# RWKV and RG-LRU blocks of the first stage: the short block first instead of last, three parts that end with the thirds of the tokens, and each part's chained part finished within the part

## The chip, the cores and the metric

The kernel runs on one core of a Trainium2 chip. The metric is the time of one execution on the device in microseconds, the median over several runs. One execution was recorded by the hardware profiler; its trace gives a start and a duration for each instruction on the five engines: TensorE (PE; PEld are its weight loads), VectorE (DVE), ScalarE (ACT), GpSimd (POOL) and SyncE (SP, which here issues the DMAs).

## The reference

One layer over 2064 tokens (16 learned ones ahead of 2048), model width 1024, all in fp32:

```
p  = rms_norm(h, norm_mix_pre) @ w_in
oa = rg_lru_group(xa, ya, ...)              # width 256: conv of 4, two gates, a linear scan over tokens
ob = forgetting_attention_group(q, k, v, f) # 8 heads of 64, causal, with a decay per head
oc = rwkv7_group(pc, ...)                   # 4 heads of 64, state S (64 x 64) per head:
#   S = S * w_t - (S kk_t) (kk_t a_t)^T + v_t k_t^T ;  o_t = S r_t ;  then group norm, bonus, gate
h  = h + rms_norm(concat([oa, ob, oc]) @ w_out, norm_mix_post)
f  = causal_dwconv(rms_norm(h, norm_ffn_pre) @ ffn_up, ffn_conv)     # width 2 x 2816
h  = h + rms_norm((gelu(gate) * val) @ ffn_down, norm_ffn_post)
```

`oa` and `oc` are recurrences over the tokens; everything else is matrix work.

## The kernel before

**First stage.** The tokens are cut into three thirds, which end at tokens 784, 1552 and 2064, each of two blocks of columns (400 + 384, 384 + 384, 256 + 256). For each third the tokens are normalised and transposed (line 145 is the transpose on TensorE, line 132 the last step of the norm on VectorE), and then projected through `w_in` in units of 128 output columns. A projection unit is made of split products, three matmuls for each fp32 one (lines 177 to 179), into the PSUM tile `psp`; there are 1152 of them in each third by the program. Lines 296 and 297 are the forget gate's small projection (`psf`).

**Recurrences beside it.** RWKV runs in nine blocks, b0 to b8, of chunks of 64 tokens: `Rwkv.block(b)` is a generator, and a step of it is what lies between two `yield`s. Block b begins at token `start(b)`. b0 to b7 have four chunks and b8 has one. A block has two parts. The first goes up to `SOLVED`: the block's *front* (loads, line 1075 the decay's products, 1105 the keys' normalisation, 1126 the bonus), the *scores* of each chunk (1149, 1154, with the transposes of line 1185), and the *rounds* that solve 16 x 16 triangles, 15 on GpSimd (line 1204) and VectorE (1205) by turns. The second, called here the block's *ending* (e0 to e8), is the chained part: it reads the solved triangles back (1218), combines them in many 32 x 32 matmuls (1234), forms the chunks' products (1278 to 1322), carries the state from chunk to chunk (1330 on TensorE, 1334 on VectorE) into the outputs (1361, 1366), normalises them (1371 to 1398, with lines 1386 and 1390 on TensorE) and stores them (1400). PSUM tiles of the recurrences are `rps` and `eps`. Some tiles of the rounds exist once and are used again by the next block's front, so the matmul of line 1105 for block b+1 comes after the rounds of block b.

The function `recurrences` strings this together: for a third, two steps of gates, then for each of three blocks the part up to `SOLVED`, the *previous* block's ending (kept in `R.ending`), and the RG-LRU block of the same tokens (`lru_block`, lines 1474 to 1508, with matmuls 1481 and 1482). `Beside` advances it: from the fourteenth projection unit of each third it makes 1.25 steps for each block of columns of a unit, and what is left goes on in the next third. After the last third `beside.finish()` runs the rest and a loop runs the last ending.

**What comes next.** The recurrences' pools are closed and the attention starts (`Attn.run`). Its half 0 takes the first two blocks of 512 queries of all heads, its half 1 the others. Line 704 and 705 are scores (`sc`), 576 and 578 the products for the maxima (`mx`), 591 transposes, 727 the output (`po`), 783 and 784 the denominators. For half 1 a further key buffer (`k2`, a constant part filled by the casts of line 499 on VectorE, the keys loaded at lines 537 to 541) and small buffers (`mt`) lie in the memory that the recurrences' pools had. Then follow `w_out` and the feed-forward part.

**Order.** The program's text does not fix the order on an engine: a scheduler with a model of times reorders the instructions of the whole program within their dependences, and so score matmuls of the attention stand among the recurrences' last matmuls.

Of the kernel before, what the change touches and what calls it, by code (L numbers as in the profile page):

```python
# [21 lines left out]
META = 16  # L22
# [204 lines left out]


def w_in_step(core, pools, psum, weights, block, kind, c0, scr):

    nc = core.nc
# [217 lines left out]
class Attn:  # L449
# [54 lines left out]
    def next(self, s):  # L504
        self.turn[s] = (self.turn[s] + 1) % len(self.ring[s])
        return self.ring[s][self.turn[s]]
# [165 lines left out]
    def weights(self, h, b, keys, queries, fill):  # L672
# [19 lines left out]
        def group_scores(group):  # L692
# [23 lines left out]
            return out  # L716

        def group_values(group, ps_, start, end):

            if start:  # L720
# [194 lines left out]
CH = 64  # L915
# [87 lines left out]
class Rwkv:  # L1003
# [6 lines left out]
    @staticmethod  # L1010
    def start(b):

        return META - CH + 4 * CH * b

    def __init__(self, core, pool, dpool, psum, epsum, scr, k):
        self.core, self.pool, self.dpool, self.psum, self.epsum = core, pool, dpool, psum, epsum
# [28 lines left out]
            nc.vector.scalar_tensor_tensor(out, v(raw[:, p, :n]), k["mu"][:, cc], out, op0=ALU.mult, op1=ALU.add)  # L1045

    def block(self, b):
        nch = 4 if b < 8 else 1
        n = CH * nch
        m2 = 2 * nch  # L1050
        c0 = PAD + self.start(b)
        nc, k = self.nc, self.k
# [78 lines left out]
    def chunks(self, b, nch, sg, rav, bk, wc, bon):  # L1131
# [3 lines left out]
        nc, k, core = self.nc, self.k, self.core  # L1135
# [177 lines left out]


        st = k["st"]
        nc.vector.tensor_copy(st[:, 0], st[:, 4])
        gain = self.ps().rearrange("p (c a t) -> p c a t", a=2, t=64)
        for c in range(nch):
            for h in range(2):
# [793 lines left out]
def recurrences(core, R, lk, f_bias, scr, blocks, part):  # L2113


    for blk in blocks:
        gate_block(core, R, f_bias, scr, blk[2])
        yield
    for b in ((0, 1, 2), (3, 4, 5), (6, 7, 8))[part]:
        gen = R.block(b)  # L2120
        while next(gen) != R.SOLVED:
            yield
        yield from R.ending
        R.ending = gen
        yield from lru_block(core, R, scr, lk, b)


_INS = [
# [9 lines left out]
def hybrid_block_kernel(ctx: ExitStack, tc: tile.TileContext, args, out):  # L2138
    a = {s: v[0] if s != "meta_tokens" else v for s, v in args.items()}
    nc = tc.nc  # L2140
# [23 lines left out]
    with ExitStack() as p1:  # L2164
# [7 lines left out]
        with ExitStack() as p1a:  # L2172
# [6 lines left out]
            for part in range(3):  # L2179
# [10 lines left out]
                if part == 0:  # L2190
# [17 lines left out]
                    R = Rwkv(core, rp, dp, ps_rw, ps_ae, scr, rk)  # L2208
# [15 lines left out]
                if part < 2:  # L2224
                    following = w_in_norm(core, pools, ps_mm, x, meta, g_pre, part + 1)
        beside.finish()
        for _ in R.ending:
            pass
        rec.close()
        p2 = ExitStack()  # L2230
        ps_wo = [pool(p2, "ps_wo", 2, space=PSUM, **right)]
# [192 lines left out]
```

## Time and profile before

| | |
|---|---|
| median of 3 runs | 2971.63 us (2969.79 to 2985.59) |
| profiled execution | 2975.74 us, its span 2974.0 us |
| mean clock granted to TensorE | 0.979 of full speed |
| TensorE busy | 2852.4 us, 96% of the span |
| VectorE, ScalarE, GpSimd busy | 69%, 51%, 43% |
| first third's last projection matmul, next third's first | 284.9 us, 327.3 us |
| last projection matmul | 855.2 us |
| first matmul of the attention | 873.7 us |
| last matmul of the recurrences | 1091.9 us |
| first maxima of the attention's half 1 | 1104.0 us |

The times of the last four rows are starts, counted from the start of the span. A row of the trace names the engine, the line of the program and the operation, as out<-in with the tiles' names; fp32 matmuls leave two records each. In brackets stands how long the engine was idle before and what it waited for.

### The profile page before, as it was taken

To read this page: it belongs to the slowest core of one execution; us is meant where nothing else is said; L and a number is where in the kernel's file an instruction comes from. 1 tells how busy PE (TensorE), PEld (TensorE's weight loads), DVE (VectorE), ACT (ScalarE), POOL (GpSimd) and SP (SyncE) were. 2 spreads that over 40 slices of the span, in tenths; PEclk is the share of its full clock that TensorE was granted. 3 is DMA by queue.
4 is the path that set the end of the run, shared out by engine and by line. 5 is a ranking of instruction groups with operands and counts; after the bars stand their busy time and mean duration, and the time that the engine had idled before them with its cause. 6 is when DMAs were issued, how large, how long until landed. Compare 5 with 4: busy or idle time off the path is not lost.

```text
span 2974.0 us, 53306 instructions
## 1 busy us (share of the span) xinstructions
PE 2852.4 (96%) x18826; PEld 2444.3 (82%) x18826; DVE 2039.5 (69%) x3977; ACT 1503.8 (51%) x2937; POOL 1285.9 (43%) x1555
## 2 busy tenths in 40 slices
PE   6999999999988889999999999999999999999998
PEld 6998899888866555666568999999999999787887
DVE  5257754665677775566656998888778787646766
ACT  4246432554346655455644665666565665324333
POOL 1001121132114566667722667455655444646443
PEclk9999899999988999999999999999999999999999
DMA  6776479576653358445245665577777764436453
GB/s 216 237 231 220 144 250 320 182 245 218 217 125 81 88 116 229 106 98 136 64 130 189 203 193 175 165 230 211 208 211 219 218 198 138 150 114 221 146 173 121
DMA packets 470344, 530.52 MB, mean 178 GB/s; under 512 B 86862, under 2 KB 356888, under 8 KB 468524
## 3 DMA queue, kind: packets, MB, share of 16 engines
q1 hardware_dynamic: 469308, 526.18, 58.8%
q8 instruction: 148, 2.42, 0.3%
q14 instruction: 120, 0.98, 0.1%
q0 software_dynamic: 768, 0.93, 0.1%
HBM read 368.07 MB, written 158.90 MB: 177 GB/s over the span
## 4 chain that ended last, share of the span: by engine, by line
PE 75%; DVE 8%; DMA 7%; ACT 4%; issue 2%; POOL 2%; SPq 1%; DVEq 0%; POOLq 0%; ACTq 0%
PE psu L177 9%; PE psu L178 9%; PE psu L179 9%; PE psp L179 4%; PE psp L178 4%; PE psp L177 4%; PE psd L177 4%; PE psd L178 4%; PE psd L179 4%; PE po L727 4%; PE pswo L177 2%; PE pswo L178 2%; PE pswo L179 2%; PE sc L704 2%; PE mx L576 2%
## 5 line engine op out<-in xcount | busy, mean ns | idle before, releaser
L178 PE MATMUL psu<-xo,uw 128*128 128x344 f32 x1848 | 591.5, 320 | 0.0
L177 PE MATMUL psu<-xo,uw 128*128 128x344 f32 x1848 | 586.2, 322 | 2.4 <-DVE vb L1889 1.9
L179 PE MATMUL psu<-xo,uw 128*128 128x344 f32 x1848 | 582.0, 320 | 0.3 <-DVE uw L1698 0.3
L177 PE MATMUL psp<-xh,wh 128*128 128x384 f32 (+2 forms) x1152 | 378.7, 329 | 1.4 <-DMA wh<-scr_wk 1.0
L179 PE MATMUL psp<-xh,wl 128*128 128x384 f32 (+2 forms) x1152 | 376.8, 328 | 0.6 <-DMA wl<-scr_wk 0.6
L178 PE MATMUL psp<-xl,wh 128*128 128x384 f32 (+2 forms) x1152 | 375.3, 326 | 0.0
L1698 DVE TENSOR_TENSOR uw<-uq,uw 128x512 fp32r<-128x512 f32 x341 | 320.2, 944 | 59.1 <-ACT uw L1697 55.9
L177 PEld LDWEIGHTS psu<-xo,uw 128*128 128x128 f32 x1848 | 345.9, 188 | 4.2 <-DVE vb L1889 3.0
L178 PEld LDWEIGHTS psu<-xo,uw 128*128 128x128 f32 x1848 | 347.2, 188 | 0.0
L179 PEld LDWEIGHTS psu<-xo,uw 128*128 128x128 f32 x1848 | 345.7, 188 | 1.1 <-DVE uw L1698 1.1
L1697 ACT ACTIVATE uw<-uq 128x512 fp32r<-128x512 f32 x462 | 288.1, 627 | 94.8 <-PE psu L179 44.9
L709 ACT ACTIVATE p<-sc,bias 128x512 f32<-128x512 f32 (+4 forms) x352 | 197.5, 589 | 172.1 <-PE sc L705 142.1
L581 DVE TENSOR_REDUCE mc<-mx 128x1 f32<-128x512 f32 (+6 forms) x352 | 190.7, 567 | 116.7 <-PE mx L576 77.5
L1837 DVE SCALAR_TENSOR_TENSOR uy<-psu,ffn_cols,uy 128x342 f32<-128x342 f32 (+1 forms) x390 | 220.9, 568 | 60.3 <-ACT uy L1835 58.6
L1845 POOL TENSOR_TENSOR uy<-uy,uy 128x342 f32<-128x342 f32 (+1 forms) x132 | 145.1, 1099 | 232.5 <-DVE uy L1837 61.0
L1698 POOL TENSOR_TENSOR uw<-uq,uw 128x512 fp32r<-128x512 f32 x121 | 183.1, 1513 | 133.3 <-ACT uw L1697 111.9
L179 PEld LDWEIGHTS psp<-xh,wl 128*128 128x128 f32 x1152 | 218.6, 190 | 8.9 <-issue 6.2
L177 PEld LDWEIGHTS psp<-xh,wh 128*128 128x128 f32 x1152 | 218.4, 190 | 8.4 <-issue 4.4
L178 PEld LDWEIGHTS psp<-xl,wh 128*128 128x128 f32 x1152 | 218.3, 189 | 7.2 <-issue 5.7
L748 POOL TENSOR_TENSOR acc<-acc,p 128x512 f32<-128x512 f32 (+3 forms) x186 | 198.8, 1071 | 46.8 <-ACT p L709 21.3
L1698 DVE TENSOR_TENSOR fo<-u,fo 128x896 fp32r<-128x896 f32 x88 | 101.6, 1154 | 130.9 <-ACT fo L1697 130.3
L1697 ACT ACTIVATE fo<-u 128x896 fp32r<-128x896 f32 x88 | 81.3, 923 | 207.1 <-PE psd L179 116.0
(490 smaller groups left out, 6339.4 us busy)
## 6 DMA issues: line engine op xcount, KB each, us to landing
uq<-scr_us SPq DMA_DIRECT2D x220, 256.0 KB
uq<-in_ffn_up_dram SPq DMA_DIRECT2D x209, 256.0 KB
wl<-scr_wk SPq DMA_DIRECT2D x48, 512.0 KB
wh<-scr_wk SPq DMA_DIRECT2D x48, 512.0 KB
u<-scr_ff SPq DMA_DIRECT2D x88, 256.0 KB
scr_ff<-uy SPq DMA_DIRECT2D x110, 171.0 KB
raw<-in_w_in_dram SPq DMA_DIRECT2D x24, 512.0 KB
scr_wk<-wh SPq DMA_DIRECT2D x24, 512.0 KB
```

What stands on the lines that cost most here:

```text
L177: nc.tensor.matmul(out, ah, bh, start=first, stop=False, skip_group_check=more)
L178: nc.tensor.matmul(out, ah, bl, start=False, stop=False, skip_group_check=more)
L179: nc.tensor.matmul(out, al, bh, start=False, stop=last, skip_group_check=more)
L576: nc.tensor.matmul(ps[:rows, : e - a], q3[:, qo : qo + rows], k2[:, a:e], start=True, stop=not last)
L581: self.reduced = nc.vector.tensor_reduce(mc[:rows, i, ci : ci + 1], ps[:rows, : e - a], axis=AX.X, op=ALU.max)
L709: last = nc.scalar.activation(p[:rows, :w], ps[:rows, :w], AF.Exp, bias=bias[:rows, j : j + 1])
L727: mm = nc.tensor.matmul(po[at : at + 64, c0:n], v1[:rows, j], p[:rows, : n - c0], start=start and i < 2, stop=end and i + 2 >= len(group), ...
L748: eng.tensor_tensor(a, ps_[0][0][:rows, c0:n] if start and i == 1 else a, p[:rows, : n - c0], op=ALU.add)
L1697: core.nc.scalar.activation(hi, src, AF.Copy)
L1698: (eng or core.nc.vector).tensor_tensor(lo, src, hi, op=ALU.subtract)
L1837: core.conved = stt(y[:, :n], src[:, i : n + i], cw[:, 44 * i + cc : 44 * i + cc + 1], y[:, :n], op0=ALU.mult, op1=ALU.add)
L1845: core.pooled = nc.gpsimd.tensor_tensor(v[:, :n], g[:, :n], v[:, :n], op=ALU.mult)
```

## The change

The short block of one chunk becomes b0 instead of b8. Blocks 1 to 8 have four chunks each and begin at tokens 16, 272, ... 1808, so that b3 ends at token 784, b6 at 1552 and b8 at 2064, where the thirds end. The state is copied on from column 1 after the short block. The three parts of `recurrences` have four, three and two blocks instead of three each, and each part ends with the ending of its last block; before, that ending was left for the next part, or for the loop behind the last one, which goes. In steps the parts have 74, 56 and 38 instead of 46, 56 and 56 with 10 behind them.

```diff
@@ -1010,7 +1010,7 @@
     @staticmethod
     def start(b):
 
-        return META - CH + 4 * CH * b
+        return META + 4 * CH * (b - 1) if b else META - CH
 
     def __init__(self, core, pool, dpool, psum, epsum, scr, k):
         self.core, self.pool, self.dpool, self.psum, self.epsum = core, pool, dpool, psum, epsum
@@ -1045,7 +1045,7 @@
             nc.vector.scalar_tensor_tensor(out, v(raw[:, p, :n]), k["mu"][:, cc], out, op0=ALU.mult, op1=ALU.add)
 
     def block(self, b):
-        nch = 4 if b < 8 else 1
+        nch = 4 if b else 1
         n = CH * nch
         m2 = 2 * nch
         c0 = PAD + self.start(b)
@@ -1313,7 +1313,7 @@
 
 
         st = k["st"]
-        nc.vector.tensor_copy(st[:, 0], st[:, 4])
+        nc.vector.tensor_copy(st[:, 0], st[:, 1 if b == 1 else 4])
         gain = self.ps().rearrange("p (c a t) -> p c a t", a=2, t=64)
         for c in range(nch):
             for h in range(2):
@@ -2116,13 +2116,15 @@
     for blk in blocks:
         gate_block(core, R, f_bias, scr, blk[2])
         yield
-    for b in ((0, 1, 2), (3, 4, 5), (6, 7, 8))[part]:
+    for b in ((0, 1, 2, 3), (4, 5, 6), (7, 8))[part]:
         gen = R.block(b)
         while next(gen) != R.SOLVED:
             yield
         yield from R.ending
         R.ending = gen
         yield from lru_block(core, R, scr, lk, b)
+    yield from R.ending
+    R.ending = ()
 
 
 _INS = [
@@ -2224,8 +2226,6 @@
                 if part < 2:
                     following = w_in_norm(core, pools, ps_mm, x, meta, g_pre, part + 1)
         beside.finish()
-        for _ in R.ending:
-            pass
         rec.close()
         p2 = ExitStack()
         ps_wo = [pool(p2, "ps_wo", 2, space=PSUM, **right)]
```

The change moves instructions at three places that matter for what follows. In the rows, `<-` stands between what is written and what is read, and xN counts matmuls in a row.

On TensorE between the first third's projection and the second's, before, in the middle of that place: `rps` rows of line 1234 and on are e0, with four chunks, `eps` rows of line 1075 are the front of b2, `pst` rows the transposes of the next tokens.

```order
L1234 MATMUL rps_2389<-rwxu_2339,rwsc_1646 32x32 x32
L1234 MATMUL rps_2465<-rwxu_2339 32x32 x16
L1234 MATMUL rps_2484<-rwxu_2339 32x32 x32
L1234 MATMUL rps_2558<-rwxu_2339,rwsc_1646 32x32 x16
L1075 MATMUL eps_3380<-rwwa_3361,wa_up 128x256 x2
L1234 MATMUL rps_2623<-rwxf_2387,rwxu_2339 32x32 x16
L1278 MATMUL rps_2642<-rww_202_1647,rwsc_1646 64x64 x16
L1075 MATMUL eps_3386<-rwwa_3361,wa_up 128x256 x2
L145 MATMUL pst_3272<-ident,xt_3257 128x128 x4
L145 MATMUL pst_3279<-ident,xt_3257 128x128 x4
L1289 MATMUL rps_2693<-rww_202_1647,rwxf_2387 64x128 x8
```

After the change, from e0's later rows to its last matmuls of line 1366:

```order
L1234 MATMUL rps_2455<-rwxu_2296,rwsc_1646 32x32 x4
L1086 MATMUL eps_3172<-rwsq_3169,gat 4x256 x2
L1234 MATMUL rps_2508<-rwxf_2344,rwxu_2296 32x32 x4
L1278 MATMUL rps_2515<-rww_202_1647,rwsc_1646 64x64 x4
L1289 MATMUL rps_2554<-rww_202_1647,rwxf_2344 64x128 x4
L1310 MATMUL rps_2603<-rwsc_1646,rwxu_2553 64x128 x4
L1322 MATMUL rps_2611<-rww_202_1647,rwsc_1646 64x64 x4
L1330 MATMUL rps_2611<-rstate,rwgt_2601 64x64 x4
L1361 MATMUL rps_2654<-rstate,rwrav_1626 64x64 x2
L1366 MATMUL rps_2654<-rww_202_1647,rwsc_1646 64x64 x2
L1361 MATMUL rps_2662<-rstate,rwrav_1626 64x64 x2
L1366 MATMUL rps_2662<-rww_202_1647,rwsc_1646 64x64 x2
```

e0 now has one chunk, a quarter of the matmuls in each of its groups, and it is over, group norm apart, ahead of the last transposes; ahead of that place nothing stands of line 1185, as b1's scores come later. Altogether 197 `rps` matmuls stood between the two thirds' projections, and 56 do now.

On TensorE at the end of the last third's projection, before: e5 is in its middle (lines 1310 to 1361), with the front of b7 (1105, 1126) beside it.

```order
L177 MATMUL psp_10273<-xh_6689,wh_9991 128x256
L178 MATMUL psp_10273<-xl_6690,wh_9991 128x256
L179 MATMUL psp_10273<-xh_6689,wl_9992 128x256
L1310 MATMUL rps_9403<-rwsc_7458,rwxu_9339 64x128 x8
L1105 MATMUL eps_9889<-rwix_9833,spr 128x256 x2
L1310 MATMUL rps_9414<-rwsc_7458,rwxu_9339 64x128 x8
L1322 MATMUL rps_9426<-rww_961_7459,rwsc_7458 64x64 x16
L1330 MATMUL rps_9426<-rstate,rwgt_9401 64x64
L1126 MATMUL eps_9919<-rwsq_9826,bones 128x512
L1330 MATMUL rps_9426<-rstate,rwgt_9401 64x64 x3
L1361 MATMUL rps_9464<-rstate,rwrav_7410 64x64
L1330 MATMUL rps_9426<-rstate,rwgt_9401 64x64 x4
```

After, at the same place:

```order
L178 MATMUL psp_10797<-xl_7032,wh_10575 128x256
L179 MATMUL psp_10797<-xh_7031,wl_10576 128x256
L1390 MATMUL rps_8587<-rwsg_6547,g_up 128x256
L1234 MATMUL rps_8854<-rwxu_8799,rwsc_7870 32x32 x32
L1481 MATMUL eps_9855<-rwlu_9847,lru_ga_w 128x256
L1482 MATMUL eps_9855<-rwlu_9847,lru_gx_w 128x256
L1234 MATMUL rps_8916<-rwxu_8799 32x32 x16
L1234 MATMUL rps_8935<-rwxu_8799 32x32 x32
L704 MATMUL sc_11454<-q_1434_11365,k_1424_11324 128x512
L704 MATMUL sc_11460<-q_1434_11365,k_1424_11324 128x400
L1234 MATMUL rps_9007<-rwxu_8799,rwsc_7870 32x32 x16
L1481 MATMUL eps_9963<-rwlu_9955,lru_ga_w 128x256
```

After the change the row of line 1390 is the end of e5, and e6 begins (1234) behind the last projection matmul, as far as the attention's first scores and beyond. Further on in the attention, e6 ends at score matmul 29 of half 0, b7's transposes (1185) stand at 40 and the next matmul of the recurrences, line 1105 of b8, at 88; e7 goes to 160 and e8 to 208. Before, e6 went from 39 to 88, e7 from 96 to 151 and the short e8 to 190, without such a hole.

On TensorE at the end of the recurrences, before: the last group norm's matmuls (1386, 1390, with one chunk of 64 columns) and what follows them. The first maxima of half 1 (line 576 with `k_1937`) come 32 rows behind the first one.

```order
L1386 MATMUL rps_11294<-ident,rwxu_11255 128x64
L1390 MATMUL rps_11296<-rwsg_10604,g_up 128x64
L704 MATMUL sc_13080<-q_1826_12730,k_1429_11337 128x272
L705 MATMUL sc_13080<-q_1433_11348,k_1430_11338 128x272
L704 MATMUL sc_13086<-q_1826_12730,k_1429_11337 128x144
L705 MATMUL sc_13086<-q_1433_11348,k_1430_11338 128x144
L576 MATMUL mx_13046<-k_1430_11338,q_1427_11331 128x512
```

```order
L727 MATMUL po_13102<-p_13083,v_1431_11343 64x272
L727 MATMUL po_13102<-p_13089,v_1431_11343 64x144
L727 MATMUL po_13102<-p_13099,v_1431_11343 64x16
L576 MATMUL mx_13162<-k_1937_13112,q_1432_11344 128x400
L576 MATMUL mx_13165<-k_1937_13112,q_1432_11344 128x512
```

After:

```order
L727 MATMUL po_13102<-p_13083,v_1431_11343 64x272
L727 MATMUL po_13102<-p_13089,v_1431_11343 64x144
L727 MATMUL po_13102<-p_13099,v_1431_11343 64x16
L704 MATMUL sc_13273<-q_1896_12975,k_1429_11337 128x512
L704 MATMUL sc_13278<-q_1896_12975,k_1429_11337 128x512
L1386 MATMUL rps_11285<-ident,rww_1316_10196 128x128 x2
L1390 MATMUL rps_11288<-rwsg_10025,g_up 128x256
L1386 MATMUL rps_11293<-ident,rww_1316_10196 128x128 x2
L1390 MATMUL rps_11296<-rwsg_10025,g_up 128x256
L576 MATMUL mx_13162<-k_1937_13112,q_1432_11344 128x400
L576 MATMUL mx_13165<-k_1937_13112,q_1432_11344 128x512
```

The score and output matmuls of half 0 that stood between the last row of line 1390 and the maxima of half 1 now stand ahead of it, and the maxima follow it at once.

## The prediction

> Times below run from the start of the profiled span, in us; e0 to e8 are the endings (chained parts) of the blocks b0 to b8, in the order in which they run. "Counts by the order" come from the order of instructions on TensorE before and after, "solved" is the end of a block's 15 rounds on GpSimd and VectorE.
>
> **What bounds the kernel now.** I read the page first: its line of TensorE, then the chain of work that ended last.
>
> ```profile
> PE 2852.4 (96%) x18826; PEld 2444.3 (82%) x18826; DVE 2039.5 (69%) x3977; ACT 1503.8 (51%) x2937; POOL 1285.9 (43%) x1555
> PE 75%; DVE 8%; DMA 7%; ACT 4%; issue 2%; POOL 2%; SPq 1%; DVEq 0%; POOLq 0%; ACTq 0%
> ```
>
> TensorE is busy 96% of the span, so work that merely moves costs nothing, and only its idle time is to be had. The busy time by stretches shows where that lies: from the end of the first third's projection to the next one's start (285 to 327.5), the other two thirds, the attention's half 0 with what is left of the recurrences (855.5 to 1104, called the tail), and half 1 with what follows.
>
> ```profile
> core 0: us, PE busy (x) PEld busy (x) DVE busy (x) ACT busy (x) POOL busy (x), PEclk, DMA share, GB/s
> 285.00:327.50 42.50, 34.48 (x473) 29.06 (x472) 33.41 (x94) 30.16 (x63) 11.01 (x22) 0.76 0.35 111
> 327.50:855.50 528.00, 513.69 (x5083) 466.60 (x5082) 319.91 (x824) 225.63 (x463) 111.42 (x178) 0.99 0.70 225
> 855.50:1104.00 248.50, 209.91 (x1984) 138.48 (x1983) 190.32 (x531) 139.38 (x311) 125.05 (x204) 0.88 0.46 106
> 1104.00:1200.00 96.00, 87.96 (x416) 48.36 (x418) 58.49 (x118) 45.37 (x82) 60.42 (x71) 0.92 0.73 198
> ```
>
> The projection is bound by TensorE (513.69 of 528). The boundary has 8 us of idle time, the tail 38.6. What sets the tail's length is seen in TensorE's timeline:
>
> ```profile
> 855.24 0.28 PE L179 MATMUL psp<-xh,wl 128*128 128x256 f32 x1
> 873.70 1.10 PE L704 MATMUL sc<-q,k 128*128 128x512 f32 x2 [0.88 <-DMA q<-scr_qh]
> 901.68 0.59 PE L1390 MATMUL rps<-rwsg,g_up 128*128 128x256 f32 x2
> 902.99 1.16 PE L1149 MATMUL rps<-rwrav,rwbk 64*128 64x128 f32 x8
> 922.86 0.75 PE L1234 MATMUL rps<-rwxu,rwsc 32*32 32x32 f32 x64
> 988.85 0.59 PE L1390 MATMUL rps<-rwsg,g_up 128*128 128x256 f32 x2
> 996.91 0.75 PE L1234 MATMUL rps<-rwxu,rwsc 32*32 32x32 f32 x64 [0.71 <-ACT rwsc L1187]
> 1055.70 0.38 PE L1390 MATMUL rps<-rwsg,g_up 128*128 128x256 f32 x1
> 1058.23 0.33 PE L1234 MATMUL rps<-rwxu,rwsc 32*32 32x32 f32 x16 [0.82 <-DVE rww L1398]
> 1091.89 0.43 PE L1390 MATMUL rps<-rwsg,g_up 128*128 128x64 f32 x2
> 1103.98 0.77 PE L576 MATMUL mx<-k,q 128*128 128x400 f32 x3 [1.68 <-DMA k<-scr_cl]
> ```
>
> From the projection's last matmul to half 1's first maxima the recurrences follow one another without a gap: the rest of e5 46.4, b7's scores to e6's first matmul 21.2, e6 66.0, b8's scores 8.1, e7 58.8, a step 2.5, the short e8 33.7, and a hand-off of 12.1, together 248.7. The hand-off is the preparation of half 1's keys, in buffers that lie where the recurrences' lay:
>
> ```profile
> 1094.89 3.29 DVE L499 CAST k<-ident 64x520 fp32r<-64x520 f32 x4
> 1097.67 0.59 SPq L537 DMA_DIRECT2D k<-scr_kh  x1
> ```
>
> The casts follow the last group norm on VectorE, the keys' loads follow the casts on SyncE's queue, the maxima wait for the loads.
>
> **The change part by part.** *Work leaves the projection.* By the order 115 fewer matmuls of the recurrences' tile rps stand ahead of the projection's last one (1574 to 1459), and three more of eps (120 to 123); in the tail it is the other way round. The traces split a program's matmul in two, so the prices are twice those of one record, rps first, then eps:
>
> ```profile
> 288.00:327.00 39.00, 16.03 (x370) 14.03 (x370) 6.30 (x16) 7.49 (x19) 0.74 0.34 109
> 327.00:855.50 528.50, 112.08 (x2526) 90.52 (x2526) 59.57 (x138) 43.84 (x106) 0.99 0.70 225
> 855.50:1104.00 248.50, 66.93 (x1278) 53.18 (x1278) 33.17 (x91) 20.02 (x52) 0.88 0.46 106
> ```
>
> ```profile
> 327.00:855.50 528.50, 42.24 (x151) 22.12 (x149) 16.56 (x40) 18.40 (x44) 0.99 0.70 225
> 855.50:1104.00 248.50, 10.14 (x40) 5.93 (x40) 4.01 (x11) 4.14 (x12) 0.88 0.46 106
> ```
>
> One rps costs 2 × 112.08/2526 = 0.089 us beside the projection, one eps 0.56: -115 × 0.089 + 3 × 0.56 = -8.5 us.
>
> *The boundary loses its filling.* Before, e0 of four chunks fills TensorE there; after it has one chunk. By the order 197 rps stood between the two projections, and now 56: 141 × 2 × 16.03/370 = 12.2 us less, and 15 of 32 forget-gate matmuls come behind the next third's first (0.175 us apart in the timeline, 2.6 us). If all 14.8 us shorten it, the gain of 8.5 stays whole. If the norm of the last two tiles keeps its length, the end of the projection is 14.8 - 8.5 = 6.3 us later. The row that decides:
>
> ```profile
> 308.76 1.97 PE L145 MATMUL pst<-ident,xt 128*128 128x128 f32 x8 [0.62 <-DVE xt L132]
> 314.11 1.09 PE L145 MATMUL pst<-ident,xt 128*128 128x128 f32 x8
> ```
>
> The transposes wait for VectorE's norm although TensorE has e0 to do. From 314.11, 1 us for the last tile and 17 × 0.175 = 3 us reach 318 instead of 327, so I take 9 of the 14.8: the projection ends 3 us earlier (-8.5 to +6.3).
>
> *A hole in the chain.* Ending each third's chain early leaves nothing to do while the next block is solved. Before, e(b-1) filled the wait behind b's transposes. Now e6 starts right at the projection's end, and between b7's transposes (40 score matmuls into the attention) and b8's first dependent matmul, L1105 (88), no recurrence matmul stands. What that wait lasts, first and last round of b7 on GpSimd, then L1105 of b8; and what L1105 to L1149 takes where nothing holds it:
>
> ```profile
> 920.86 0.24 POOL L1204 TENSOR_TENSOR rwitmp<-rwix,rwia 128x16 f32<-128x16 f32 x1
> 948.73 0.52 POOL L1204 TENSOR_TENSOR rwitmp<-rwix,rwia 128x128 f32<-128x128 f32 x1 [0.70 <-DVE rwix L1205]
> 961.56 0.65 PE L1105 MATMUL eps<-rwix,spr 4*128 4x64 f32 x4
> 198.49 1.12 PE L1105 MATMUL eps<-rwix,spr 4*128 4x256 f32 x4
> 207.07 0.48 PE L1149 MATMUL rps<-rwrav,rwbk 64*128 64x128 f32 x2
> ```
>
> That is 27.9 + 12.8 + 8.6 us. The same hole behind b4 (before b5, 227 projection matmuls long) is covered by the projection, which is TensorE-bound; if that cover were gone it would cost its 27.9 + 12.8.
>
> *The tail, from above.* With a serial chain: e6 62.4 (mean of 66.0 and 58.8), b7's scores 17.9 (902.99 to 920.86), the hole 49.3, b8's scores now full-sized like b7's 19.9 (902.99 to 922.86), e7 58.8, step 2.5, e8 now full 58.8, hand-off 12.1: 281.7, or +33.
>
> *The tail, from below.* TensorE's work becomes 209.91 + 115 × 2 × 66.93/1278 - 3 × 2 × 10.14/40 = 220.4. Its stretches:
>
> ```profile
> 855.50:873.70 18.20, 9.96 (x92) 6.89 (x91) 15.98 (x43) 2.59 (x8) 0.31 (x1) 0.72 0.44 110
> 873.70:901.70 28.00, 25.27 (x153) 18.05 (x154) 19.20 (x58) 9.69 (x21) 7.36 (x12) 0.57 0.90 187
> 901.70:1091.90 190.20, 166.64 (x1702) 109.40 (x1700) 148.87 (x419) 119.93 (x266) 108.63 (x178) 0.93 0.39 94
> 1091.90:1104.00 12.10, 8.05 (x42) 4.15 (x41) 6.27 (x13) 7.17 (x18) 8.75 (x15) 1.00 0.52 104
> ```
>
> The opening, while the first keys load, stays 18.2 with its 10 us of work. The hand-off stays 12.1, but its 8.05 us of score and output matmuls stand ahead of the last L1390 after the change, with nothing between it and the maxima. The other 210.4 us go without any wait in 210.4: 240.7, or -8. At the 88% of the third row (166.64 of 190.20) they take 240: 270. The chain and the third row agree within 12 us, the floor has no row that runs so full, so I take 267, a little less than 270 because the hole leaves the attention alone for a while: +18.5.
>
> *What costs nothing.* The step counts (74, 56 and 38 for 46, 56, 56 and 10 afterwards) only move work already counted; the state copy from column 1 and the parts' lists are the same instructions. Stores of blocks (L1400) are nine before and after. Behind the maxima the order is the same but for a few neighbours: 0, unless the clock is lower there.
>
> On the clock: the stretch from 873.70 was granted 0.57 although TensorE was busy 25.27 of 28 us, behind an opening with 8 us of waits. The Trainium skill, "TensorE: Matmul & The Clock Gate" (Part 1, What's actually happening), says that the clock halves after an idle window of about 3.4 us and is released after as long a busy one. By that rule an uncovered hand-off of 12 us, longer than the window, makes half 1 start at half clock and costs some 1.7 us (an estimate from that page); this trace's drop agrees with the rule, its 28 us do not. By the row it is up to 0.43 × 28 = 12 us, of which the half-1 row (0.92 of 96 us) already pays 7.7 now, so up to 4 more, kept for the range.
>
> *Sum.* -3 + 18.5 = +15.5. The profiled execution took 2975.74 and the median is 2971.63, 4.1 less; the difference is added to the median: 2987.
>
> **The rivals.** *Faster:* the tail runs at its floor. Its place is the hole: attention alone may fill TensorE wholly, as the projection does (97%), and then the endings are off the path. Price: -8 and -8.5, 2955. For it speaks that e7's and e6's times include 55 and 49 score matmuls beside them; against it, that no stretch of this tail longer than 20 us shows it, and that the rows above hang together without slack. It decides once the last L1390 comes within 229 us of the projection's end (now 236.7).
>
> *No difference to be told (0.5%, 15 us, is about what these runs can tell):* the waits of the chain shrink by half because e6 runs with fewer neighbours and the rounds in the hole meet a freer GpSimd. Then 210.4 us at 93% are 226, the tail 256.5, +8; with -3 the time is 2977. Here belongs that the change does not do what its counts promise: 14 steps are left after the projection instead of 36, yet by the order three endings stand beside the attention after it, as (nearly) before.
>
> *Much slower:* the chain stays wholly serial, +33, and the boundary keeps its length, +6: 3011, and half 1 starts cold. The full e8 as the last piece and b8's scores alone are 25.1 + 11.8 of it.
>
> **How the numbers follow.** The forecast (TensorE in the tail no fuller than now, 2987, own range 2976 to 2999) has 0.45, much slower 0.15, no difference 0.25, faster 0.15. The forecast lies at the bound of 0.5% (2986.5): I give somewhat over two thirds of it to slower, since its unknown costs reach further up. Slower: 0.32 + 0.15 = 0.47; same: 0.13 + 0.25 - 0.02 = 0.36, 0.02 of it going to faster for a floor nearly reached: 0.17. The range goes from the faster case's 2955 to 3006, short of the serial chain's whole price; about 2 in 10 lie outside.
>
> **What would show it.** The projection's last matmul at 846 to 862 (forecast 852). On TensorE e6's first L1234 right behind it; some 40 us without recurrence matmuls between b7's L1185 and b8's L1105; the last L1390 255 us after the projection's end, not 237; half 1's first maxima 12 us behind it, waiting for keys with TensorE idle for most of that. I am wrong if the hole is filled at over 95% and e8 takes no longer than 45 us, or if the boundary shortens by its whole 14.8 us.

## The result and the profile after

The changed kernel takes 3013.16 us (median of 4 runs, 3010.19 to 3018.12) against 2972.94 us of the kernel before (median of 4 runs): ratio 1.0129, 95% interval 1.0096 to 1.0162. Run again beside the kernel before on one chip it took 3005.92 against 2978.11 us, 1.0102 (1.0078 to 1.0126). The forecast, slower at 2987 us, had the direction; the time lies 7 us above its range (2955 to 3006). The profiled execution of the changed kernel is the slowest of its four, 3018.12 us with a span of 3016.4.

TensorE's line of the page and the chain that ended last, after:

```profile
PE 2865.0 (95%) x18826; PEld 2452.5 (81%) x18826; DVE 2029.2 (67%) x3977; ACT 1511.7 (50%) x2937; POOL 1291.9 (43%) x1555
PE 77%; DMA 7%; DVE 6%; ACT 3%; POOL 3%; issue 2%; SPq 2%; DVEq 0%; POOLq 0%; ACTq 0%
```

The same matmuls kept TensorE busy 12.6 us longer in a span that is 42.4 us longer: some matmuls ran slower, and 30 us were added in which it waits. Where, is read from the busy time by stretches. Of the kernel before first: the first third, the boundary behind it, the second third, the place behind that, the last third's projection.

```profile
0.00:284.60 284.60, 260.66 (x1446) 244.76 (x1447) 154.00 (x418) 118.20 (x213) 23.14 (x51) 0.99 0.71 225
284.60:327.00 42.40, 34.38 (x474) 29.22 (x472) 33.77 (x95) 29.66 (x63) 11.01 (x22) 0.76 0.35 111
327.00:609.20 282.20, 278.21 (x2370) 253.02 (x2369) 160.60 (x401) 105.98 (x206) 55.13 (x82) 1.00 0.73 240
609.20:616.60 7.40, 6.87 (x53) 5.99 (x51) 5.78 (x15) 4.69 (x10) 2.56 (x4) 1.00 1.07 372
616.60:855.30 238.70, 228.91 (x2665) 207.82 (x2664) 153.34 (x410) 115.46 (x248) 53.73 (x93) 0.99 0.64 204
```

After, the same five, and the tail up to half 1's first maxima:

```profile
0.00:275.00 275.00, 251.32 (x1416) 239.76 (x1417) 144.40 (x432) 114.99 (x224) 26.71 (x57) 1.00 0.70 226
275.00:312.00 37.00, 24.72 (x190) 18.76 (x189) 33.95 (x103) 23.44 (x49) 9.22 (x16) 0.68 0.44 144
312.00:633.30 321.30, 307.73 (x2782) 278.78 (x2781) 184.55 (x479) 134.70 (x262) 56.29 (x87) 0.96 0.66 215
633.30:644.30 11.00, 11.00 (x106) 10.04 (x105) 9.42 (x16) 5.33 (x11) 3.32 (x5) 1.00 1.06 385
644.30:874.50 230.20, 216.97 (x2300) 198.75 (x2300) 131.77 (x352) 90.61 (x196) 53.67 (x88) 0.96 0.63 199
874.50:1148.00 273.50, 221.93 (x2201) 144.14 (x2199) 189.51 (x489) 149.79 (x310) 131.46 (x213) 0.85 0.44 103
```

The five stretches changed by -9.6, -5.4, +39.1, +3.6 and -8.5 us, so the projection ends 19 us later, and the tail is 25 us longer (273.5 against 248.5). Behind it little changed: from half 1's first maxima to `w_out` it takes 74.8 us instead of 72.3, and from there to the end 1793 instead of 1798. In the second third TensorE has 29.5 us more busy time and 9.6 us more waits (13.6 against 4.0), at a granted clock of 0.96 instead of 1.00; in the last third it has 12 us less busy time, but 3.4 us more waits, at 0.96 instead of 0.99. What it waited for in the second third, after, with the total, the number and the longest; then before:

```profile
PE psp L177 <- DMA wh<-scr_wk: 7.8, 3, 3.0
PE psp L179 <- DMA wl<-scr_wk: 1.6, 1, 1.6
```

```profile
PE psp L177 <- DMA wh<-scr_wk: 1.0, 1, 1.0
PE psp L179 <- DMA wl<-scr_wk: 0.6, 2, 0.3
```

The projection's weights come late. One such wait, on SyncE's queue and on TensorE, and the clock around it; the first row is the last matmul of the unit before the one that runs as the loads are issued:

```profile
495.19 0.34 PE L179 MATMUL psp<-xh,wl 128*128 128x384 f32 x1
496.60 4.67 SPq L1218 DMA_DIRECT2D rwxu<-dx  x7
501.69 0.34 SPq L245 DMA_DIRECT2D scr_kh<-sth  x1
...
503.55 0.99 SPq L1537 DMA_DIRECT2D raw<-in_w_out_dram  x1
504.64 1.01 SPq L225 DMA_DIRECT2D wh<-scr_wk  x1
...
508.00 0.69 SPq L225 DMA_DIRECT2D wh<-scr_wk  x1
511.03 0.44 PE L177 MATMUL psp<-xh,wh 128*128 128x384 f32 x1 [2.92 <-DMA wh<-scr_wk]
500.00:522.00 22.00, 18.17 (x152) 0.84 0.75 255
```

The queue issues without a pause here: the loads of a block's solved triangles (line 1218), stores of keys, `w_out`'s rows, and only then two pairs of weights. TensorE waits for the first pair (the second is that of the next unit). In the second third the weights have two buffers of their own, and the one that this load fills was read for the last time by the first row's matmul, over at 495.5; the load was issued 9.1 us later, when its turn came. So here the order on the queue makes the weights late, and not the buffer. The longest wait, 3.0 us at 354.4, is of the same kind: the buffer is free at 340.3, the queue issues eight stores of line 1172 (`da`) from 339.7 to 344.5 and more behind them, and the load follows at 347.6. The wait of 2.9 us is followed by matmuls at half clock, 0.84 on the mean of 22 us.

The tail, TensorE's timeline after (last projection matmul, e6, b7's scores, b8 from line 1105 on, e7, e8, half 1), with the first and last round of b7 on GpSimd:

```profile
874.52 0.28 PE L179 MATMUL psp<-xh,wl 128*128 128x256 f32 x1
875.17 0.75 PE L1234 MATMUL rps<-rwxu,rwsc 32*32 32x32 f32 x64
946.59 0.59 PE L1390 MATMUL rps<-rwsg,g_up 128*128 128x256 f32 x2
947.29 1.16 PE L1149 MATMUL rps<-rwrav,rwbk 64*128 64x128 f32 x8
962.03 0.24 POOL L1204 TENSOR_TENSOR rwitmp<-rwix,rwia 128x16 f32<-128x16 f32 x1 [1.45 <-DVE rwia L1199]
983.22 0.51 POOL L1204 TENSOR_TENSOR rwitmp<-rwix,rwia 128x128 f32<-128x128 f32 x1
1000.75 1.13 PE L1105 MATMUL eps<-rwix,spr 4*128 4x256 f32 x4
1006.55 0.48 PE L1149 MATMUL rps<-rwrav,rwbk 64*128 64x128 f32 x2
1023.62 0.85 PE L1234 MATMUL rps<-rwxu,rwsc 32*32 32x32 f32 x64
1086.42 0.59 PE L1390 MATMUL rps<-rwsg,g_up 128*128 128x256 f32 x2
1087.90 0.75 PE L1234 MATMUL rps<-rwxu,rwsc 32*32 32x32 f32 x64
1137.41 0.66 PE L1386 MATMUL rps<-ident,rww 128*128 128x128 f32 x2 [4.95 <-DVE rww L1379]
1139.76 1.22 PE L1390 MATMUL rps<-rwsg,g_up 128*128 128x256 f32 x2 [0.30 <-DVE rww L1398]
1148.34 1.31 PE L576 MATMUL mx<-k,q 128*128 128x400 f32 x3 [7.36 <-DMA mt<-scr_qh]
1223.09 0.42 PE L177 MATMUL pswo<-woh,mh 128*2 128x512 f32 x1
```

The chain is serial, as forecast: e6 72.1 from the projection's end, b7's scores 15.4, the hole 44.5 (962.03 to 1006.55, in which TensorE does attention alone up to 1000.75), b8's scores 17.1, e7 62.8, a step 1.5, e8 51.9, and a hand-off of 8.6, of which TensorE waits 7.4. The row puts this wait down to a load of `mt`, but its matmul reads the keys, whose loads stand just ahead of that one on SyncE's queue (1141.9 to 1144.3). `w_out` begins 83.3 us behind the last matmul of the recurrences; before, the two stand at 1091.89 and 1176.30, 84.4 apart.

### The profile page after: what moved, and what is told of

It reads as the page before. It is cut to its first block, busy times and chain, and to the rows that moved or that the text cites. A ratio compares the mean times of both kernels' runs of the same rounds, so it can differ in the third digit from the quotient of the medians.

```text
span 3016.4 us, 53330 instructions
## 1 busy us (share of the span) xinstructions
PE 2865.0 (95%) x18826; PEld 2452.5 (81%) x18826; DVE 2029.2 (67%) x3977; ACT 1511.7 (50%) x2937; POOL 1291.9 (43%) x1555
## 4 chain that ended last, share of the span: by engine, by line
PE 77%; DMA 7%; DVE 6%; ACT 3%; POOL 3%; issue 2%; SPq 2%; DVEq 0%; POOLq 0%; ACTq 0%
PE psu L177 9%; PE psu L178 9%; PE psu L179 9%; PE psp L177 5%; PE psp L179 5%; PE psp L178 5%; PE psd L177 4%; PE psd L178 4%; PE psd L179 4%; PE po L727 4%; PE pswo L177 2%; PE pswo L178 2%; PE pswo L179 2%; PE sc L704 2%; PE mx L576 2%
## 5 line engine op out<-in xcount | busy, mean ns | idle before, releaser
L178 PE MATMUL psp<-xl,wh 128*128 128x384 f32 (+2 forms) x1152 | 381.6, 331 | 0.0
```

What stands on the lines that cost most here:

```text
L178: nc.tensor.matmul(out, ah, bl, start=False, stop=False, skip_group_check=more)
```

## The experiments

The runs have numbers; e0 to e8 are still the endings of the blocks. All were timed beside the kernel before on the same chip. Starts in each one's profile: the projection's last matmul, the recurrences' last (line 1390), `w_out`'s first, and the distance of these two.

| run | projection's end | recurrences' end | w_out | distance | ratio to before (95%) |
|---|---|---|---|---|---|
| before | 855.2 | 1091.9 | 1176.3 | 84.4 | |
| 10, before again | 854.9 | 1091.1 | 1172.9 | 81.8 | 0.9999 (0.9987 to 1.0010) |
| after | 874.5 | 1139.8 | 1223.1 | 83.3 | 1.0129 (1.0096 to 1.0162) |
| 9, after again | 865.9 | 1125.2 | 1207.7 | 82.5 | 1.0102 (1.0078 to 1.0126) |
| 1, no early endings | 878.8 | 1051.3 | 1174.8 | 123.5 | 1.0001 (0.9985 to 1.0017) |
| 2, early endings alone | 874.6 | 1115.9 | 1199.3 | 83.4 | 1.0036 (1.0023 to 1.0049) |
| 3, short block first alone | 854.1 | 1126.5 | 1212.9 | 86.4 | 1.0100 (1.0085 to 1.0116) |
| 4, run 3 with early endings | 856.7 | 1135.0 | 1221.5 | 86.4 | 1.0129 (1.0108 to 1.0151) |
| 5, only ending e3 early | 861.6 | 1087.5 | 1194.3 | 106.8 | 1.0045 (1.0029 to 1.0060) |
| 6, only ending e6 early | 888.2 | 1113.2 | 1200.4 | 87.3 | 1.0037 (1.0025 to 1.0049) |
| 7, `w_out`'s rows later | 913.6 | 1123.0 | 1217.5 | 94.5 | 1.0096 (1.0080 to 1.0112) |
| 8, sums later | 860.0 | 1118.6 | 1259.1 | 140.5 | 1.0233 (1.0217 to 1.0248) |
| 11, run 1 with pace 1.5 | 901.7 | 1059.2 | 1196.5 | 137.3 | 1.0023 (1.0010 to 1.0036) |
| 12, run 1 with pace 1.1 | 854.2 | 1070.8 | 1191.1 | 120.3 | 1.0039 (1.0024 to 1.0054) |
| 13, after, loads by ScalarE | 869.7 | 1126.9 | 1208.5 | 81.6 | 1.0072 (1.0054 to 1.0090) |
| 14, before, loads by ScalarE | 878.5 | 1095.5 | 1199.4 | 103.9 | 1.0080 (1.0063 to 1.0096) |
| 15, run 1, loads by ScalarE | 887.8 | 1052.5 | 1182.0 | 129.5 | 1.0014 (1.0003 to 1.0024) |

In nine profiles the distance is 81.6 to 87.3 us: there half 1 begins when the recurrences end. In the other eight (94.5 and more) their end no longer decides.

**Run 1, without the early endings.** Blocks and parts as changed.

```diff
         yield from lru_block(core, R, scr, lk, b)
-    yield from R.ending
-    R.ending = ()
...
         beside.finish()
+        for _ in R.ending:
+            pass
         rec.close()
```

> The changed kernel without its early endings: blocks and parts as changed, but each part's last ending is carried on into the next part, and the very last one runs behind the projection, as before the change. Theory A (the late end of the projection comes from crowding the second third, which has 808 rps matmuls by the order here, 774 in the changed kernel, 583 before; the long tail comes from the early endings, which leave holes in the chain): the projection ends at 868 to 876 as in the changed kernel; the recurrences' last matmul stands at score matmul 142 of half 0 instead of 208, so half 1's keys are ready in time and the tail is 225 to 240 us; in all 2965 to 2985 us. Rival B (the early endings cause both): the projection ends at 853 to 860, in all 2945 to 2965. Rival C (a full-sized last ending is what lengthens the tail): tail 265 to 280, in all 3000 to 3015.

```profile
878.83 0.28 PE L179 MATMUL psp<-xh,wl 128*128 128x256 f32 x1
1051.33 0.59 PE L1390 MATMUL rps<-rwsg,g_up 128*128 128x256 f32 x2
1086.62 0.53 PE L576 MATMUL mx<-k,q 128*128 128x400 f32 x2 [1.83 <-DVE mt L493]
1174.78 0.42 PE L177 MATMUL pswo<-woh,mh 128*2 128x512 f32 x1
```

As late a projection as in the changed kernel (4 us later), but the recurrences end 89 us earlier (1051.3 against 1139.8), although their last ending is full-sized here too, and half 1 no longer waits for them. The whole loss is gone: theory A by its time; B and C are out. The tail, 208 us, is shorter than any of the theories had it. But late weights are not the reason here. All that TensorE waited for them in the second third (312.2 to 629.6):

```profile
PE psp L177 <- DMA wh<-scr_wk: 2.1, 1, 2.1
```

With 225 rps matmuls more than before (808 against 583) the second third is 35 us longer here, 30 of which are the work at the prediction's prices. So a crowded second third need not make the weights late.

**Run 2, the early endings alone**, on the old blocks and parts (the lines that run 1 takes out and puts back, the other way round in the kernel before).

> The kernel before with the early endings alone: blocks and parts as before, each part ends with its last block's ending. Theory A: the second third has 621 rps matmuls by the order (before 583), so the projection ends at 853 to 862; the tail has the hole (b7's transposes ahead of the projection's last matmuls, line 1105 of b8 at score matmul 20) but a short last ending, and half 1's maxima follow the last ending at once with the keys' 12 us uncovered: tail 250 to 265; in all 2972 to 2992 us. Rival B (the early endings cause both delays): projection at 868 to 878, tail 265 to 280, in all 3000 to 3020. Rival C (the full-sized last ending is the cause): tail 245 to 250, in all 2968 to 2978.

2988.0 us. The early endings cost 0.4% here. Theory A had the time but not its parts: the projection ends 19 us later, as rival B had it, and the tail is no longer than before. (The profiled execution, 2995.2 us, is 7 us above the median.) The second third and the place behind it held 709 rps matmuls by the order against 583, so their hold on the projection is not a matter of the short block.

**Runs 3 and 4, three blocks in each part**, without and with the early endings.

```diff
-    for b in ((0, 1, 2, 3), (4, 5, 6), (7, 8))[part]:
+    for b in ((0, 1, 2), (3, 4, 5), (6, 7, 8))[part]:
```

> The short block first, but three blocks in each part and endings carried on as before the change. By the order the second third has 538 rps matmuls (583 before, 774 in the changed kernel), the third one 746, the tail 840, and the last ending, a full one, ends at score matmul 207. Theory A: with the second third uncrowded the projection ends at 840 to 853; the tail has 184 rps matmuls more than before at 0.105 us and uncovered keys: 270 to 285; in all 2985 to 3005 us. Rival B (early endings cause both): projection as before, tail 250 to 260, in all 2970 to 2982. Rival D (the short first block itself lengthens the projection, by the emptier boundary): projection at 865 to 875, in all 3000 to 3025.

> The short block first and the early endings, but three blocks in each part: the changed kernel with only its lists of parts undone. Second third 568 rps matmuls, third one 730, tail 778, last matmul of the recurrences at score matmul 208. Theory A: projection at 842 to 856, tail 268 to 282 as in the changed kernel (274), in all 2988 to 3006 us. Rival B (the early endings cause the late projection): projection at 868 to 878, in all 3008 to 3025. Rival C (full last ending sets the tail): the same tail as without the early endings.

3006.64 and 3016.87 us, 2 and 11 us above theory A's ranges. With 538 and 568 rps matmuls in the second third the projection ends within 1.5 us of the kernel before, so neither the short first block nor the emptier boundary holds it up: D is out. So is B with these starts, though in run 2, with the old ones, its number for the projection came. What is not done by then lengthens the tail instead, to 272 and 278 us up to the recurrences' end (before 237). That run 4's tail is about that of run 3 agrees with C, which run 1 has ruled out. The new parts are worth 1.0% where endings are carried on (run 3 to run 1), and at most 0.3% where they are early (run 4 to the changed kernel).

**Runs 5 and 6, one early ending each**: e3 at the end of the first part (run 5), or e6 at the end of the second (run 6). The last part's stays in both, where it is the same as the loop before the change.

```diff
-    yield from R.ending
-    R.ending = ()
+    if part != 1:            # run 6: if part:
+        yield from R.ending
+        R.ending = ()
```

> The changed kernel, with the early ending of the second part alone carried on into the third part (e6); the early ending of the first part (e3, with nothing left to fill b4's rounds) stays. Theory E (an early ending is paid for where it leaves a hole, and the hole behind b7 in the attention, not the size of the last ending, makes the tail long): the projection ends as in the changed kernel (872 to 877, the order there is the same: 774 and 555 rps in the second and third third), but e6 now stands behind b7's scores and fills its rounds, the recurrences end at score matmul 158 instead of 208, 215 to 235 us after the projection, and the keys of half 1 are covered; in all 2978 to 2996 us. Rival C (the full last ending sets the tail): last matmul of the recurrences 260 us after the projection's end or later, in all 3005 to 3016.

> The changed kernel, with the early ending of the first part alone carried on (e3 runs beside b4); that of the second part (e6 ahead of b7's rounds) stays. By the order 808 and 754 rps matmuls in the second and third third, 562 in the tail, and a hole from score matmul 12 to 64 behind b7's transposes. Theory E: projection ends at 876 to 884; despite 209 rps fewer in the tail than in the changed kernel, the last matmul stands at score matmul 198 and the keys are hardly covered: tail 240 to 262, in all 2990 to 3012 us. Rival (holes cost nothing, the tail goes by its amount of work): 656 - 562 = 94 rps fewer than before are 10 us less, tail 235 to 240, in all 2983 to 2990.

```profile
861.63 0.28 PE L179 MATMUL psp<-xh,wl 128*128 128x256 f32 x1
1087.45 0.70 PE L1390 MATMUL rps<-rwsg,g_up 128*128 128x256 f32 x2
1194.27 0.42 PE L177 MATMUL pswo<-woh,mh 128*2 128x512 f32 x1
```

```profile
888.21 0.28 PE L179 MATMUL psp<-xh,wl 128*128 128x256 f32 x1
1113.17 0.59 PE L1390 MATMUL rps<-rwsg,g_up 128*128 128x256 f32 x2
1200.42 0.42 PE L177 MATMUL pswo<-woh,mh 128*2 128x512 f32 x1
```

From the projection's end to the recurrences' end run 1 takes 172 us, runs 5 and 6 take 226 and 225, and the changed kernel with both endings early 265 (run 9: 259): each early ending adds some 50 us, and the two some 90, about a hole (44.5) each. In run 5 part of this is work, as its tail holds 771 rps matmuls against run 1's 602; in run 6 it holds 562 and is longer all the same. In run 5 the full last ending stands, the hole behind b7 is filled, and the keys are covered; C is out again. In run 6 the rival gave the tail better than theory E (235 to 240, measured 235 to half 1's maxima at 1122.9), but holes do cost, as the comparison with run 1 shows; the projection ended later still. Up to the projection's end run 5's order is that of the changed kernel but for a few matmuls late in the last third, and it ended 13 us sooner: one profile tells that time to no better than this, hence the next two.

**Runs 9 and 10, both kernels again**, unchanged.

> The changed kernel once more, for a second profile and for times on one chip beside the kernel before. Theory H (the late end of the projection, 874, is in part the luck of one execution: the version with only e6 carried on has the same order up to there and ended at 862): the end lies between 860 and 876, the second third still waits 6 to 10 us for the weights wh and wl; w_out still begins 82 to 87 us after the recurrences' last matmul, as in all versions whose last ending stands directly ahead of half 1; in all 1.0 to 1.5% slower than before. Rival: the projection ends at 874 within 3 us again, the early ending of the second part then costs the projection 12 us although it stands behind it.

> The kernel before once more: how far the stages move between two executions of one kernel. Projection's end at 852 to 860, last matmul of the recurrences 232 to 242 us after it, w_out's first matmul 82 to 87 us behind that; ratio 0.998 to 1.002.

The kernel before is repeated within 1 us up to the recurrences' end. The changed kernel's projection ended at 865.9; weights were waited for 8.4 us in the second third (9.4 in the first profile). So it ends 6 to 19 us later than in the kernel before, 12 on the mean of the three profiles (after, 9 and 5).

**Runs 7 and 8, less on SyncE's queue in the second third**: the preparation of `w_out` or the sums of the feed-forward weights wait for the last third.

```diff
-                    if part == 1 and i > 1:
+                    if part == 2 and i > 1:        # run 7
...
-                    if part and i % 2 == 0:
+                    if part == 2 and i % 2 == 0:   # run 8
```

> The changed kernel with the preparation of w_out (loads, two stores of each of 8 rows, on SyncE's queue) moved from the second third to the third one; the work on TensorE is the same. Theory F (in the second third SyncE's queue has too much to issue between its waits, so the projection's weights come late: 9.4 us of TensorE's waits for them and the lower clock behind each): waits for wh and wl below 4 us in the second third, which takes 303 to 312 us instead of 321; the third one longer by 5 to 15. In all 2990 to 3012 us. Rival G (the weights are late because of the traffic of the recurrences or because the buffers come free late, not by the queue): second third 317 to 325 us, waits as before.

> The changed kernel with the sums of the feed-forward weights (GpSimd, with a load and a store each on SyncE's queue; the store waits for GpSimd, 18.7 us in the second third) left to the third third and its end. Theory F: waits for wh and wl below 4 us in the second third, its length 303 to 313 instead of 321; the third third pays with waits of its own. Rival G: second third 317 to 325. In all 2985 to 3020 us, since 10 sums then follow the last unit; by the order the recurrences end at score matmul 114.

The second third, runs 7 and 8, and all that TensorE waited for weights in it:

```profile
312.00:616.60 304.60, 296.91 (x2775) 0.99 0.58 179
313.40:616.90 303.50, 298.97 (x2778) 0.99 0.58 191
PE psp L179 <- DMA wl<-scr_wk: 1.0, 2, 0.6
PE psp L177 <- DMA wh<-scr_wk: 0.8, 1, 0.8
```

With TensorE's work as it was but for 4 and 2 eps matmuls, it takes 304.6 and 303.5 us instead of 316 to 321, waits 1.0 and 0.8 us for weights, and the clock is back at 0.99: the late weights and the clock behind them are 11 to 18 us (8 against run 5's second third, 312.7). This takes it that the other order on TensorE, which the scheduler chose in both runs, is worth nothing, and that is not shown. Run 8 pays more than that later (its attention waits 42.2 us for its first queries). Run 7 pays about as much, and its total is that of the changed kernel: its last third takes 283.5 us, with 19.7 us of waits for weights; in that third half of the pairs of weights share buffers with `w_out`'s rows.

**Runs 13, 14 and 15, line 1218's loads issued by ScalarE**: in the changed kernel, the kernel before, and run 1's version.

```diff
-                nc.sync.dma_start(
+                nc.scalar.dma_start(
                     xt[64 * h + 16 * q : 64 * h + 16 * q + 16, ...
```

> The changed kernel with the eight loads of a block's solved triangles (line 1218) issued by ScalarE instead of SyncE; same transfers, same buffers, TensorE's order the same up to the projection's end. If SyncE's queue makes the weights late: waits for wh and wl in the second third below 4 us (before 8 to 9), the second third 303 to 312 us instead of 316 to 321, the projection's end 852 to 864; the tail as before this edit; in all 2985 to 3003 us. If it is buffers or traffic: waits of 6 us and more, second third 313 to 321.

> The kernel before with the same edit. Its weights are hardly late (1.6 us), so the projection ends at 850 to 858; by the order the recurrences end at score matmul 166 instead of 190, so w_out may begin earlier: 2960 to 2978 us, ratio 0.994 to 1.001. If the loads by ScalarE hold up its own work: 1.002 to 1.008.

> Without the early endings, and the loads of line 1218 issued by ScalarE. The second third has little to gain in waits for weights (3 us), the recurrences end at score matmul 130 instead of 142, which no longer decides: ratio to before 0.994 to 1.001. If SyncE's queue cost more than the waits show (lower clock): 0.988 to 0.994, and this version beats both kernels.

Waits for weights in the changed kernel's second third fall from 9.4 and 8.4 to 5.2 us, its length to 312.8: between the two theories. Its two longest waits, at 354 and 511, are gone; but TensorE's order is not the same here, though that had been expected. In the kernel before the waits rise from 1.6 to 5.6 us and its projection ends 23 us later; its ratio, 1.008, is that of the alternative (ScalarE's own work held up), which was not looked into. Run 15 gains nothing: 1.0014 is just above its range. So the queue's order makes the two longest waits of the changed kernel; whether queue or traffic makes the others stays open.

**Runs 11 and 12, run 1 with another pace**, the two attempts at a version that beats the kernel before.

```diff
-PACE = 1.25
+PACE = 1.5        # run 12: 1.1
```

> Without the early endings as in the first experiment, and with 1.5 steps of the recurrences for each block of columns instead of 1.25. By the order 53 rps matmuls more stand ahead of the projection's end (767 in the last third, before 714) and 549 instead of 602 behind it, the recurrences end at score matmul 123 instead of 142. If the end of the recurrences no longer decides (theory: w_out began 123 us behind it at 1.25 steps), nothing more is gained: 2960 to 2985 us, ratio to before 0.996 to 1.004. If the chain's end still decides, w_out begins some 8 us earlier: ratio 0.994 to 0.998.

> Without the early endings as in the first experiment, and with 1.1 steps of the recurrences for each block of columns instead of 1.25. By the order the second third has 616 rps matmuls instead of 808, the place behind it 64, the last third 673 instead of 714, the tail 771 instead of 602, and the recurrences end at score matmul 151 instead of 142. Theory A with F (crowding the second third brings late weights and a lower clock; the recurrences' end has some 35 us to spare without the early endings): waits for the weights under 4 us, the projection ends at 848 to 864 instead of 879, the recurrences' end 225 to 245 us behind it, w_out 88 us or more behind that; 2955 to 2975 us, ratio to before 0.993 to 0.999. Rival (what leaves the projection only lengthens the tail by as much): ratio 0.999 to 1.004. If the chain's end decides again (w_out 82 to 87 us behind it): 1.004 to 1.010.

Neither gains. At 1.5 the projection ends at 901.7 and the recurrences 137 us ahead of `w_out`, to no use. At 1.1 the projection ends where it did before the change, with 3.7 us of waits for weights, and `w_out` still begins 16 us later than at 1.25: what leaves the projection comes back in the tail, the rival. No version here is faster than the kernel before.

## Why the prediction was wrong, point by point

- **The projection's end is the step that failed**: -3 us forecast (-8.5 to +6.3), +19 and, in run 9, +11 measured. This is 22 of the 27 us by which the profiled executions miss the forecast (+42.4 against +15.5); the tail has 6.5 more, and 2 came back behind it. By stages, in us:

| stage | at the prediction's prices | after | run 9 |
|---|---|---|---|
| first third (16 rps fewer) | -1.4 | -9.6 | -9 |
| boundary (9 of 14.8 taken) | -9 | -5.4 | -5 |
| second third (191 rps, 10 eps, 15 forget-gate matmuls more) | +25 | +39.1 | +33 |
| place behind it (24 rps more) | +2 | +3.6 | +4 |
| last third (rps and eps fewer) | -19.5 | -8.5 | -12 |

  I priced moved work at its average cost beside the projection and held the projection to be bound by TensorE's work alone, "covered" wherever the chain has a hole. For the second third the price is about right while the weights come in time: runs 7 and 8 are 21 to 22 us above the kernel before. In the changed kernel 7.8 us more waits for weights (9.4 against 1.6) and a lower clock come on top; the two longest of these waits are for loads that stood behind others on SyncE's queue. More recurrence matmuls alone do not bring this about: in run 1, with still more of them, the waits are 2.1 us. In the last third no weights are late. There 3.4 us more waits and the clock (0.96 against 0.99 on 230 us, up to 7 us) are the size of what is missing, and what causes them is not shown.
- **The tail was sized rightly, in part by luck**: 267 us forecast, 273.5 and, in run 9, 268 measured. In number the estimate by TensorE's busy share (220.4 us of work in 270) came nearer, with 221.9 in 273.5, than the serial chain (281.7). The chain is the mechanism that the timeline shows, and its pieces are off in both directions, so that part of the agreement is luck: the hole took 44.5 (49.3 forecast), e6 72 (62), e8 51.9 (58.8), the hand-off 8.6 (12.1). That an early ending opens the hole, and that half 1 then waits for the keys behind a full-sized ending, is what runs 1 and 5 show. With the new starts and parts the early endings cost 1.0 to 1.3%, the whole loss: without them (run 1) the projection is as late, the recurrences' end no longer decides, and nothing is lost.
- **That nothing changes behind the maxima** nearly held: 2.5 us more to `w_out`, then 4 us less. The 4 us kept for the clock were not needed: both kernels run 10 to 12 us at the start of half 1 at half clock. The clock around the changed kernel's hand-off, its first 24 us of half 1, and the same 24 us and its slow part in the kernel before:

```profile
1136.00:1148.30 12.30, 3.27 (x8) 0.50 0.42 79
1148.30:1160.00 11.70, 10.78 (x36) 0.50 0.32 83
1148.30:1172.30 24.00, 22.64 (x94) 0.76 0.43 103
1104.00:1128.00 24.00, 22.18 (x96) 0.79 0.53 124
1105.80:1116.00 10.20, 8.93 (x31) 0.50 0.45 97
```

  After the change half clock sets in at 1136, ahead of the keys' wait, in the 5.0 us that TensorE waits for the last group norm. By the rule of the Trainium skill ("TensorE: Matmul & The Clock Gate", Part 1) half clock follows an idle window of some 3.4 us, which agrees with that wait. That it ends after as long a busy one does not agree: 11.7 us with TensorE busy for 10.78 of them passed from 1148.3 on. Nor was so long a wait needed: 2.9 us were enough at 511, and in the kernel before half clock came at 1105.8 with no wait over 1.7 us behind the recurrences' end.
- **Of the rivals**, "much slower" (3011, the serial chain and the boundary's length) came nearest, with 0.15. Its place for the additional time was wrong: the boundary shortened, and the second and the last third took it. The floor of the faster case was nowhere near: TensorE is busy 81% of the tail.

## What to carry to other kernels

A chain that is finished early at a boundary loses what filled the waits of the next piece: count what stands on the critical engine between a piece's last input and its first dependent instruction, before and after. Work moved beside a "full" stage must be priced in the stretch it lands in, with that stretch's transfers and queue, not at the stage's average, since a late weight load cost its wait here and then the clock behind it. And where a later stage's buffers come free only when a chain ends, measure the distance from the chain's end to that stage in each version: where it is constant, the chain decides.

## What the runs showed that I had not expected

The end of the projection scatters by 13 us over three profiles with nearly one order up to there (861.6, 865.9, 874.5); up to the second third's end the order is the same, and 9 us of the scatter are in that third alone. The kernel before is repeated within 0.3 us (855.2, 854.9). Moving eight small loads of each block to another engine's queue delays the kernel before by 0.8%, most of it again in the projection, which ends 23 us later.
